# Softmax over two query blocks, head norms over two tiles, and moved steps at the openings of a two-layer decoder trunk

## The chip, the cores and the metric

The kernel runs on one NeuronCore of a Trainium2 chip. The metric is the device time of one launch in microseconds (us). Five engines work beside each other, each in the order of its own queue: TensorE (PE in the profile, with its weight loads as PEld), VectorE (DVE), ScalarE (ACT), GpSimd (POOL) and SyncE (SP), which issues the DMAs. They meet through semaphores.

## The reference

Two layers over 1024 positions and 1024 features, all in float32. Layer 0 mixes with a gated linear recurrence and a matrix memory; layer 1 with sliding-window attention. After each mixer comes a gated feed-forward block with a short convolution, then a gated per-layer embedding. Cut to what the change touches:

```python
def rms_norm(x, g):
    xf = x.astype(jnp.float32)
    y = xf * lax.rsqrt(jnp.mean(xf * xf, axis=-1, keepdims=True) + EPS)
    return (y * g.astype(jnp.float32)).astype(x.dtype)

def banded_sink_attention(q, k, v, sinks):      # q: 16 heads of 64, k and v: 4 heads, blocks of 128 queries
    ...
    logits = jnp.einsum('bnqhgd,bnkhd->bnhgqk', qb, kw) * (dh ** -0.5)
    band = (kj > qi) & (kj <= qi + WINDOW)
    logits = jnp.where(valid[None, :, None, None], logits, -jnp.inf)
    m = jnp.maximum(jnp.max(logits, axis=-1), sink)
    probs = jnp.exp(logits - m[..., None])
    denom = jnp.sum(probs, axis=-1) + jnp.exp(sink - m)
    out = jnp.einsum('bnhgqk,bnkhd->bnhgqd', probs, vw) / denom[..., None]

def reference(...):
    for layer in range(DEPTH):
        h = rms_norm(x, norm_mix[layer])
        mix = rglru_mlstm_mixer(h, ...) if layer % 2 == 0 else swa_sink_mixer(h, positions, ...)
        x = x + mix
        x = x + conv_ffn(rms_norm(x, norm_ffn[layer]), ...)
        gate = jax.nn.sigmoid(rms_norm(x, norm_ple[layer]) @ ple_w_gate[layer])
        x = x + gate * (p[layer] @ ple_w_proj[layer])
```

## The kernel before

Activations lie feature-major: a page is 128 features by 1024 positions, 51 pages are handed out from a free list (`page`, `drop`). Products are made in split precision: every operand is a high part and a low part (`split_cols`: a copy on ACT, a subtraction on DVE or POOL), and a product is three matmuls of 512 columns per 128x128 block of weights. PSUM's eight banks go round in a queue (`bank`, `done`); a bank can be written again when the operation that emptied it is through. The order of the program is the order in which the Python issues it; nothing is rescheduled, and each engine takes its instructions in that order.

**Openings.** `Opening` starts a product group behind an RMS norm while that norm is still being made. `block1`, `norm2` and `block2` prepare the first 512 positions; `run` then issues eight "parts" (12 matmuls each: two pairs of weight tiles, two tiles each, two quarters of the features) and, between them, the second half's statistic `stat(1)` (transposes of the summed squares, a reduce and an inverse square root of about a dozen small DVE operations in `rsqrt`), its `spread(1)` over the partitions, the norms and the blocks 3 and 8. In the kernel before, `stat(1)` stands behind part 2 (counted from 0) and `spread(1)` with all that follows behind part 5, at every opening. After the eight parts come four tiles of two parts each, with the block sums of the fast product scheme (`diff3`, `sum2`, `diffs`) between them, and behind the last of them the blocks 5. The opening is used three times: for layer 0's input projection (with `sums=False`), and for both feed-forward blocks. In the feed-forward block the caller's loop issues the steps of the finished tile after each yield: `s1` (ACT), `s2` (taps on DVE), `s3` (GELU on ACT), `s4` (DVE).

At layer 0, `start` issues the embedding projections and the first half's norm. `first_mid`, called when the blocks 3 and 8 are issued, splits the weights of the eight gate columns (`if_weights`: two casts and two subtractions of 32 columns on DVE) and lets weight making go on. `if_products` follows behind the first finished tile, then `if_cols`, `if_log`, `if_rows`, `if_scan`, `if_rest` and `if_done` at set steps of a slot queue (`later`, `tick`). `constants`, some 30 small DVE operations and three on ACT, stands in slot 4.

**Attention.** The head tiles of `QKV` (128 features: two heads of keys, or one head each of two groups of queries) are made one after another by `qkv_part`, with a `tick` every second of eight steps. Each gets its rotation and its head norm in slots: `rot_a` (evacuation, squares, an exchange of halves by DMA), `rot_s` (transposes and sums of the squares), `rot_b`, `rot_c` (the inverse square root by `rsqrt` for one tile at a time) and, for keys, `rot_k` in slot 6, which waits on PE for the page `rb` that POOL makes in `rot_c`. `attention` is a generator of 32 units (pair of key heads P, half n, block b of 128 queries); `weave` sets one of its steps between the steps of the main products. `scores` of a unit makes the logits of four heads in two banks, folds the window's two halves into 128 columns (`copy_predicated`), takes the maximum, and lets ACT exponentiate head by head with the sum in the same instruction. `normal` (one unit later) adds the sink, takes the reciprocal and multiplies on POOL. `turn` (three units later) transposes on PE and multiplies with two masks on DVE into a page of 1024 columns; `values` (four units later) makes the product with the values.

At the attention's opening two `norm_stat` calls, each with its own chain of small operations, make the row norm `rcol`.

Of the kernel before, what the change touches and what calls it, by code (L numbers as in the profile page):

```python
# [14 lines left out]
ALU = mybir.AluOpType  # L15
# [88 lines left out]
NFIRST, LN, LT, NPOOL, D0, R0, R1 = True, 1, 3, True, 8, 1.0, 1.5  # L104
# [23 lines left out]
class Core:  # L128
# [263 lines left out]
    def rsqrt(self, v, n, name, bufs=2):  # L392

        nc = self.nc
        y = self.small(name + "y", n, bufs=bufs)
        t = self.small(name + "t", n, bufs=bufs)
# [4 lines left out]
        for _ in range(3):  # L401
            nc.vector.tensor_tensor(out=t, in0=y, in1=y, op=ALU.mult)
            nc.vector.scalar_tensor_tensor(out=t, in0=t, scalar=-0.5, in1=v, op0=ALU.mult, op1=ALU.mult)
            nc.vector.scalar_tensor_tensor(out=y, in0=t, scalar=1.5, in1=y, op0=ALU.add, op1=ALU.mult)
        return y
# [25 lines left out]
    def norm_stat(self, h):  # L431
# [10 lines left out]
        return bk, self.rsqrt(v, 4, "n")  # L442

# [242 lines left out]
def layers(ctx: ExitStack, tc: tile.TileContext, a: dict, out: bass.AP, peaks):  # L686
# [157 lines left out]
    def start(op):  # L844
# [21 lines left out]
        for t in pk:  # L866
            c.drop(*t)
        c.ahead = (4, 0)
# [62 lines left out]
    class Opening:  # L931
# [37 lines left out]
        def run(self, p0, p1, extra=None, mid=None, sums=True):  # L969
# [20 lines left out]

            for n, (p, r) in enumerate(tiles):
                p.part(r, 0, 0, True, False)
                if n == 2:
                    self.stat(1)
            for n, (p, r) in enumerate(tiles):
                p.part(r, 0, 1, False, True)
                if n == 1:
                    self.spread(1)
                    self.norm(range(4, 8), 1)
                    self.singles(3, 4, 1)  # L1000
                    c.drop(c.acc, c.sqt)
                    self.norm(range(4), 1)
                    self.singles(8, 0, 1)
                    c.done(self.rows[1])
                    if not sums:
                        c.drop(*self.xs)
                    if mid:
                        mid()
            late = deque([diff3, sum2, diffs] if sums else [])
            for p, r in tiles:  # L1010
# [110 lines left out]
    def if_rest():  # L1121
        ri, rf, rb, rm, rs = (gates[n] for n in ("ri", "rf", "rb", "rm", "rs"))
        gs, bm, ai = rs, ri, rf
        G.tensor_tensor(out=gs[0:4, :], in0=ri[0:4, :], in1=rb[0:4, :], op=ALU.subtract)
        G.tensor_tensor(out=bm[0:4, :], in0=rb[0:4, :], in1=rm[0:4, :], op=ALU.subtract)
# [3 lines left out]
        G.tensor_tensor(out=ai[0:4, :].rearrange("p (b t) -> p b t", t=128),  # L1129
# [305 lines left out]
    def first_mid():  # L1435
        if_weights()
# [397 lines left out]
    def rot_s(key, h):  # L1834

        s = Q["s", key]
        if h == 0:
            Q["v", key] = c.small("qv", 16, bufs=3)
# [3 lines left out]
        V.reduce_sum(out=Q["v", key][:, h * 8:(h + 1) * 8], in_=b.ap.rearrange("p (g d) -> p g d", d=64), axis=AX.X)  # L1842
# [4 lines left out]
    def rot_c(key):  # L1847
# [5 lines left out]
        v3 = v.rearrange("p (b s) -> p b s", s=2)  # L1853
        V.tensor_tensor(out=v3, in0=v3, in1=rcol2.unsqueeze(2).to_broadcast([128, 8, 2]), op=ALU.mult)
        V.tensor_scalar(out=v, in0=v, scalar1=1.0 / 64, scalar2=EPS, op0=ALU.mult, op1=ALU.add)
        y = c.rsqrt(v, 16, "q")
        y3 = y.rearrange("p (b s) -> p b s", s=2)
        r1 = rcol.unsqueeze(2).to_broadcast([128, 8, 2])
# [369 lines left out]
```

## Time and profile before

| | before |
|---|---|
| time, median of three runs | 2450.53 us (2445.98 to 2453.55) |
| the profiled execution's own time | 2450.45 us |
| its span in the trace | 2448.67 us |
| PE busy | 2389.4 us, 98% |
| DVE busy | 1745.3 us, 71% |
| POOL busy | 1336.0 us, 55% |
| ACT busy | 1098.4 us, 45% |
| DMA, mean | 78 GB/s |

Matmuls overlap in the profile: a matmul of 512 columns is shown with about 0.39 us, while the next starts 0.23 us after it. The granted clock (PEclk) is the share of TensorE's full clock in a stretch; it has two levels, 1.2 and 2.4 GHz, so that a stretch with 0.66 holds both.

### The profile page before, as it was taken

Reading aid. Unit: us, or ns where it says so; the run is one execution under the profiler, and the core shown is the slowest. Engines: PE = TensorE matmul, PEld = TensorE weight load, DVE = VectorE, ACT = ScalarE, POOL = GpSimd, SP = SyncE. Lnnn points to the kernel's source line nnn. Section 1 sums busy time; section 2 is a strip of 40 time slices with the busy share of each in tenths; the row PEclk is TensorE's granted clock in tenths of the full one; section 3 lists DMA queues with packets and bytes.
Section 4 is the critical chain, followed back from the end, with each engine's and each line's share of the span. In section 5 each row is a group of like instructions: output and inputs, shape, how many; then the busy total and the mean of one; then the engine's idle time right before and its main releaser. Section 6 shows DMA issues by size and latency. Waiting matters only on the chain. (4 is left out here: it accounts for less than half of the span.)

```text
span 2448.7 us, 29414 instructions
## 1 busy us (share of the span) xinstructions
PE 2389.4 (98%) x10840; PEld 1915.5 (78%) x10840; DVE 1745.3 (71%) x2569; ACT 1098.4 (45%) x1953; POOL 1336.0 (55%) x869
## 2 busy tenths in 40 slices
PE   8899999999999999999999998999999999999999
PEld 6688887877888888888887665687788888888887
DVE  6755555687777666777877888668777777667774
ACT  6474544343434434445452555535344344444441
POOL 0431203237888888888223333332788888888820
PEclk9999999999999999999999999999999999999999
DMA  7121214121111111113233113112111121111323
GB/s 272 36 90 65 78 61 176 57 95 52 52 58 64 53 60 52 52 52 130 95 132 107 31 35 121 65 65 95 52 52 52 54 68 52 61 52 52 120 78 112
DMA packets 57088, 190.18 MB, mean 78 GB/s; under 512 B 6888, under 2 KB 7400, under 8 KB 56944
## 3 DMA queue, kind: packets, MB, share of 16 engines
q1 hardware_dynamic: 56944, 188.31, 22.9%
q8 instruction: 85, 1.39, 0.2%
q14 instruction: 59, 0.48, 0.1%
HBM read 154.69 MB, written 28.34 MB: 75 GB/s over the span
## 5 line engine op out<-in xcount | busy, mean ns | idle before, releaser
L367 POOL TENSOR_TENSOR wp<-wr,wp 128x512 fp32r<-128x512 f32 x462 | 661.8, 1457 | 322.8 <-ACT wp L362 322.8
L502 PE MATMUL pb<-bh,wp 128*128 128x512 f32 x2464 | 614.2, 391 | 10.6 <-ACT u L522 8.6
L502 PEld LDWEIGHTS pb<-bh,wp 128*128 128x128 f32 x2464 | 463.9, 189 | 111.7 <-ACT u L522 9.5
L367 POOL TENSOR_TENSOR wl<-wr,wh 128x1024 fp32r<-128x1024 f32 x78 | 206.3, 2658 | 519.5 <-ACT wh L362 464.2
L616 PE MATMUL pb<-dp,wp 128*128 128x512 f32 x1848 | 457.2, 393 | 3.1 <-DVE dp L603 0.7
L620 DVE TENSOR_TENSOR x<-x,pb 128x512 f32<-128x512 f32 x616 | 398.4, 681 | 46.1 <-PE pb L616 45.9
L616 PEld LDWEIGHTS pb<-dp,wp 128*128 128x128 f32 x1848 | 341.9, 188 | 93.7 <-DVE x L620 13.3
L362 ACT ACTIVATE wp<-wr 128x512 fp32r<-128x512 f32 x462 | 270.9, 622 | 257.9 <-POOL wr L210 192.1
L502 PE MATMUL pb<-bl,wp 128*128 128x512 f32 x1232 | 330.6, 390 | 0.0
L603 DVE TENSOR_TENSOR dp<-fy,dp 128x512 fp32r<-128x512 f32 x154 | 183.2, 1190 | 146.3 <-ACT dp L600 120.7
L502 PEld LDWEIGHTS pb<-bl,wp 128*128 128x128 f32 x1232 | 232.4, 189 | 48.5
L210 POOL TENSOR_TENSOR wr<-wr,wr 128x512 f32<-128x512 f32 x154 | 227.2, 1475 | 8.9 <-DMA wr<-in_down 0.2
L600 ACT ACTIVATE dp<-fy 128x512 fp32r<-128x512 f32 x154 | 96.3, 625 | 266.3 <-DVE fy L593 99.7
L210 POOL TENSOR_TENSOR wr<-wr 128x512 f32<-128x512 f32 x110 | 162.0, 1473 | 47.1 <-DMA wr<-in_up 45.0
L1562 DVE SCALAR_TENSOR_TENSOR fy<-g,params,fy 128x1023 f32<-128x1023 f32 x96 | 156.3, 1628 | 31.9 <-ACT fy L1558 30.2
L383 PE MATMUL pb<-hh,wh 128*128 128x512 f32 x448 | 148.5, 407 | 0.0
L520 DVE TENSOR_TENSOR g<-g,pb 128x512 f32<-128x512 f32 x88 | 58.6, 684 | 125.5 <-PE pb L502 122.2
L549 PE MATMUL pb<-bh,wh 128*128 128x512 f32 x512 | 143.9, 403 | 0.0
L383 PE MATMUL pb<-hl,wh 128*128 128x512 f32 x448 | 142.6, 394 | 0.0
L383 PE MATMUL pb<-hh,wl 128*128 128x512 f32 x448 | 142.2, 393 | 0.0
L549 PE MATMUL pb<-bh,wl 128*128 128x512 f32 x512 | 137.8, 391 | 0.0
L549 PE MATMUL pb<-bl,wh 128*128 128x512 f32 x512 | 137.1, 390 | 0.0
(287 smaller groups left out, 3402.6 us busy)
## 6 DMA issues: line engine op xcount, KB each, us to landing
wr<-in_up SPq DMA_DIRECT2D x96, 512.0 KB, 3.6
wr<-in_down SPq DMA_DIRECT2D x48, 512.0 KB, 3.6
wr<-in_w_in SPq DMA_DIRECT2D x24, 512.0 KB, 5.4
x<-xd SPq DMA_DIRECT2D x24, 512.0 KB, 6.9
ppd<-pp SPq DMA_DIRECT2D x16, 512.0 KB, 3.0
wr<-in_w_out SPq DMA_DIRECT2D x16, 512.0 KB, 5.4
xd<-x SPq DMA_DIRECT2D x32, 256.0 KB, 2.0
wr<-in_gate SPq DMA_DIRECT2D x16, 512.0 KB, 3.8
```

Of the source, the lines that this page charges most:

```text
L210: self.eng(self.w_eng["sum"]).tensor_tensor(out=out, in0=a, in1=b, op=op)
L362: nc.scalar.activation(hi, src, AF.Copy)
L367: self.eng(lo_eng).tensor_tensor(out=lo, in0=src, in1=hi.bitcast(F32), op=ALU.subtract)
L383: self.nc.tensor.matmul(o, lhsT=w, rhs=x[:, c], start=(first and k == 0 and i == 0), stop=(last and k == n - 1 and i == 2))
L502: c.nc.tensor.matmul(bk.ap, lhsT=w[:, o:o + 128], rhs=self.B.t[i][k][q], start=(n == i and k == 0 and j == 0), stop=(k == 3 and j == 2), s ...
L520: c.nc.vector.tensor_tensor(out=out, in0=out, in1=bk.ap, op=ALU.add)
L549: c.nc.tensor.matmul(bk.ap, lhsT=w[n][p], rhs=x[n][q], start=(first and n == 0 and j == 0), stop=(last and n == 3 and j == 2), skip_group_ ...
L600: c.nc.scalar.activation(t[:, lo], src, AF.Copy)
L603: add(out=t[:, hi], in0=src, in1=t[:, lo].bitcast(F32), op=ALU.subtract)
L616: self.c.nc.tensor.matmul(bk.ap, lhsT=p, rhs=q, start=start and j == 0, stop=j == 2, skip_group_check=True)
L620: self.c.nc.vector.tensor_tensor(out=o, in0=o, in1=bk.ap, op=ALU.add)
L1562: V.scalar_tensor_tensor(out=y[:, s:], in0=g[:, :1024 - s], scalar=params[:, o + 2 - s:o + 3 - s], in1=y[:, s:], op0=ALU.mult, op1=ALU.add)
```

## The change

- `Opening.run` has places for the statistic and for what follows it: behind parts 0 and 2 at the feed-forward blocks, behind parts 3 and 5 at layer 0. The blocks 5 are issued ahead of the last yield, so ahead of the caller's steps for the last tile.
- `if_weights` moves from `first_mid` to the end of `start`; `constants` from slot 4 to slot 1; three operations of `if_rest` from POOL to DVE.
- At the attention's opening `norm_whole` makes both halves in one chain and writes `rcol` directly. `rsqrt` can write its last step elsewhere.
- The head norms of two query tiles are made in one chain (`rot_s`, `rot_c`): the even tile leaves its sums, the odd one goes on for both. `rot_k` of the first key tile is in slot 8 instead of 6.
- `scores` of an even block ends with the evacuation; the odd block then does maximum, sinks and exponentials for both. `normal` does nothing for even blocks and both for odd ones (two products on POOL). `turn` multiplies with both masks in one operation of 1024 columns.

```diff
-    def rsqrt(self, v, n, name, bufs=2):
+    def rsqrt(self, v, n, name, bufs=2, out=None, room=None):
...
+            z = y if out is None or i < 2 else out
+            nc.vector.scalar_tensor_tensor(out=z, in0=t, scalar=1.5, in1=y, op0=ALU.add, op1=ALU.mult)
...
+    def norm_whole(self, b, out):
+        nc = self.nc
+        self.sq_finish()
+        v = self.small("qv", 32, bufs=2)[:, :8]
+        for h in range(2):
+            for n in range(4):
+                o = h * 512 + n * 128
+                nc.tensor.transpose(b.b[h].ap[:, n * 128:(n + 1) * 128], self.acc[:, o:o + 128], self.ident)
+            nc.vector.reduce_sum(out=v[:, h * 4:h * 4 + 4], in_=b.b[h].ap.rearrange("p (b f) -> p b f", f=128), axis=AX.X)
+        nc.vector.tensor_scalar(out=v, in0=v, scalar1=1.0 / D, scalar2=EPS, op0=ALU.mult, op1=ALU.add)
+        return self.rsqrt(v, 8, "q", 1, out, 32)
...
         for t in pk:
             c.drop(*t)
+        if_weights()
         c.ahead = (4, 0)
...
-        def run(self, p0, p1, extra=None, mid=None, sums=True):
+        def run(self, p0, p1, extra=None, mid=None, sums=True, at=(0, 2)):
...
+            for n, (p, r, k) in enumerate([(p, r, k) for k in range(2) for p, r in tiles]):
+                p.part(r, 0, k, k == 0, k == 1)
+                if n == at[0]:
+                    self.stat(1)
+                if n == at[1]:
+                    rest()
...
+                if n == 3 and sums:
+                    self.B.drop(8)
+                    self.singles(5, 4, 1)
+                    c.drop(*self.xs[4:])
                 yield p, done
-            if sums:
-                self.B.drop(8)
-                self.singles(5, 4, 1)
-                c.drop(*self.xs[4:])
...
-        G.tensor_tensor(out=gs[0:4, :], in0=ri[0:4, :], in1=rb[0:4, :], op=ALU.subtract)
-        G.tensor_tensor(out=bm[0:4, :], in0=rb[0:4, :], in1=rm[0:4, :], op=ALU.subtract)
+        V.tensor_tensor(out=gs[0:4, :], in0=ri[0:4, :], in1=rb[0:4, :], op=ALU.subtract)
+        V.tensor_tensor(out=bm[0:4, :], in0=rb[0:4, :], in1=rm[0:4, :], op=ALU.subtract)
...
-        G.tensor_tensor(out=ai[0:4, :].rearrange("p (b t) -> p b t", t=128),
+        V.tensor_tensor(out=ai[0:4, :].rearrange("p (b t) -> p b t", t=128),
...
     def first_mid():
-        if_weights()
...
-    later(4, constants)
-    for p, i in op.run(in_pair(pairs0[0], Plain), in_pair(pairs0[1], Plain), gates_start, first_mid, False):
+    later(1, constants)
+    for p, i in op.run(in_pair(pairs0[0], Plain), in_pair(pairs0[1], Plain), gates_start, first_mid, False, (3, 5)):
...
         if key[1] == "q":
             P, _, r = key
-            V.tensor_tensor(out=rq6[:, P, :, r // 2, :, r % 2], in0=y3, in1=r1, op=ALU.mult)
+            if r % 2 == 0:
+                Q["vv", P] = v
+                return
+            n = 2
...
+        y = c.rsqrt(v, 16 * n, "q", 1, None, 32)
...
-                later(6, lambda: rot_k(key))
+                later(6 if key[0] else 8, lambda: rot_k(key))
...
-    st = [c.norm_stat(h) for h in range(2)]
+    b = c.wide()
+    c.norm_whole(b, rcol)
+    c.done(b)
...
+            st[u] = cb, st["cb"]
+            if b % 2 == 0:
+                return
+            cv = st["cb"].rearrange("p (b h k) -> p b h k", b=2, h=4)
...
+            V.reduce_max(out=m3, in_=cv, axis=AX.X)
+            V.scalar_tensor_tensor(out=m3, in0=m3, scalar=-1.0, in1=rr, op0=ALU.mult, op1=ALU.mult)
+            V.tensor_tensor(out=m4, in0=m4, in1=nk, op=ALU.min)
+            V.tensor_tensor(out=e4, in0=sk, in1=m4, op=ALU.add)
+            for z in range(2):
+                for h in range(4):
+                    A.activation(cv[:, z, h, :], cv[:, z, h, :], AF.Exp, bias=m3[:, z, h:h + 1], scale=rr[:, z, h:h + 1],
+                                 accum_out=sm[:, 4 * z + h:4 * z + h + 1])
...
         def normal(u):
+            if u[2] % 2 == 0:
+                return
+            cv, sm, es = st.pop("s")
             V.tensor_tensor(out=sm, in0=sm, in1=es, op=ALU.add)
             V.reciprocal(out=sm, in_=sm)
-            (G if NPOOL else V).tensor_tensor(out=cv, in0=cv, in1=sm.unsqueeze(2).to_broadcast([128, 4, 128]), op=ALU.mult)
+            for z in range(2):
+                G.tensor_tensor(out=cv[:, z], in0=cv[:, z], in1=sm[:, 4 * z:4 * z + 4].unsqueeze(2).to_broadcast([128, 4, 128]),
+                                op=ALU.mult)
...
             if b:
-                V.tensor_tensor(out=pt[:, 512:1024].rearrange("p (h q) -> p h q", h=4), in0=p3,
-                                in1=cs["prevT"].unsqueeze(1).to_broadcast([128, 4, 128]), op=ALU.mult)
+                V.tensor_tensor(out=pt.rearrange("p (z h q) -> p z h q", z=2, h=4), in0=p3.unsqueeze(1).to_broadcast([128, 2, 4, 128]),
+                                in1=masks.rearrange("p (z q) -> p z q", z=2).unsqueeze(2).to_broadcast([128, 2, 4, 128]),
+                                op=ALU.mult)
```

## Rows read from the trace of the kernel before

**Rows 1.** The page: span, and busy us (share of the span) xinstructions of the engines.
```profile
span 2448.7 us, 29414 instructions
PE 2389.4 (98%) x10840; PEld 1915.5 (78%) x10840; DVE 1745.3 (71%) x2569; ACT 1098.4 (45%) x1953; POOL 1336.0 (55%) x869
```

**Rows 2.** PE's waits, who ended them: us in total, times, longest us.
```profile
PE pb L502 <- ACT u L522: 8.6, 2, 4.3
PE pb L2004 <- DVE pt L2012: 6.5, 3, 2.6
...
PE pb L1064 <- DVE wif L367: 5.3, 2, 3.9
PE pb L1873 <- POOL rb L1865: 4.9, 1, 4.9
PE pb L438 <- DVE acc L422: 3.1, 2, 1.6
PE pb L2028 <- DVE pt L2009: 2.4, 1, 2.4
PE pb L1104 <- DVE tab L1095: 1.9, 1, 1.9
...
PE pb L1140 <- POOL rs L1124: 1.3, 1, 1.3
```

**Rows 3.** Stretches: length, busy us (xinstructions) by engine, granted clock, DMA share, GB/s.
```profile
63.00:71.50 8.50, 3.65 (x10) 0.92 (x8) 8.43 (x4) 3.45 (x5) 8.50 (x4) 0.80 0.00 0
110.00:116.00 6.00, 4.68 (x26) 3.93 (x26) 5.96 (x5) 0.00 (x0) 5.84 (x3) 0.72 0.01 3
512.00:522.00 10.00, 5.69 (x16) 4.16 (x15) 6.92 (x8) 5.17 (x9) 3.33 (x2) 0.66 0.80 292
900.00:950.00 50.00, 49.88 (x219) 40.54 (x218) 34.97 (x46) 21.42 (x36) 41.94 (x30) 1.00 0.16 53
1316.00:1328.00 12.00, 7.05 (x27) 6.01 (x27) 11.14 (x29) 0.00 (x0) 6.52 (x3) 0.72 0.23 87
1340.00:1525.00 185.00, 170.72 (x910) 116.30 (x910) 151.12 (x374) 95.92 (x321) 61.25 (x40) 0.97 0.21 63
1679.00:1689.50 10.50, 6.20 (x17) 4.58 (x17) 7.31 (x9) 5.17 (x9) 3.33 (x2) 0.67 0.76 287
```

**Rows 4.** Timeline, first feed-forward opening: start, us, engine, line, op, out<-in, idle before.
```profile
465.06 0.69 DVE L422 TENSOR_TENSOR acc<-acc,sq 128x512 f32<-128x512 f32 x1 [0.16 <-ACT sq L420]
465.09 1.07 PE L549 MATMUL pb<-bh,wh 128*128 128x512 f32 x4
...
479.80 2.72 DVE L948 SCALAR_TENSOR_TENSOR x<-x,params,pb 128x512 f32<-128x512 f32 x4 [5.54 <-PE pb L448]
...
510.40 2.61 DVE L1562 SCALAR_TENSOR_TENSOR fy<-g,params,fy 128x1023 f32<-128x1023 f32 x2
...
513.10 1.06 ACT L1567 ACTIVATE fy<-fy 128x1024 f32<-128x1024 f32 x1 [4.22 <-DVE fy L1562]
...
516.14 0.57 ACT L522 ACTIVATE u<-pb 128x512 f32<-128x512 f32 x1
```

**Rows 5.** Timeline, first opening: the gate weights' split, and POOL beside it.
```profile
61.96 9.89 POOL L367 TENSOR_TENSOR wl<-wr,wh 128x1024 fp32r<-128x1024 f32 x4 [29.00 <-ACT wh L362]
62.59 2.37 DVE L366 CAST wif<-tab 128x32 fp32r<-128x32 f32 x1
```

**Rows 6.** Timeline of POOL at the attention's opening.
```profile
1319.46 1.87 POOL L1865 TENSOR_SCALAR rb<-qy 128x1024 f32<-128x1024 f32 x1 [10.99 <-DVE qy L1863]
```

**Rows 7.** DVE by lines, 1340 to 1560 us: xcount | busy us, mean ns | idle before.
```profile
L1982 DVE TENSOR_REDUCE mx<-cb 128x4 f32<-128x512 f32 x30 | 20.6, 686 | 1.0
...
L1986 DVE TENSOR_TENSOR es<-params,mx 128x4 f32<-128x4 f32 x30 | 15.6, 520 | 1.0
...
L402 DVE TENSOR_TENSOR qt<-qy 128x16 f32<-128x16 f32 x21 | 3.7, 175 | 0.7
```

**Rows 8.** ACT by lines, 1340 to 1560 us.
```profile
L1988 ACT ACTIVATE cb<-cb,mx,tab 128x128 f32<-128x128 f32 x120 | 57.9, 483 | 91.3 <-DVE mx L1985 91.3
```

More of the change, by code (lines that the diff above doesn't have):

```diff
@@ L390, in wk @@
                 for k in range(n)]
-    def rsqrt(self, v, n, name, bufs=2):
+    def rsqrt(self, v, n, name, bufs=2, out=None, room=None):
         nc = self.nc
-        y = self.small(name + "y", n, bufs=bufs)
-        t = self.small(name + "t", n, bufs=bufs)
+        y = self.small(name + "y", room or n, bufs=bufs)[:, :n]
+        t = self.small(name + "t", room or n, bufs=bufs)[:, :n]
         nc.vector.tensor_scalar(out=t.bitcast(I32), in0=v.bitcast(I32), scalar1=1, scalar2=None,
@@ L400, in rsqrt @@
                                 op0=ALU.mult, op1=ALU.add)
-        for _ in range(3):
+        for i in range(3):
             nc.vector.tensor_tensor(out=t, in0=y, in1=y, op=ALU.mult)
             nc.vector.scalar_tensor_tensor(out=t, in0=t, scalar=-0.5, in1=v, op0=ALU.mult, op1=ALU.mult)
-            nc.vector.scalar_tensor_tensor(out=y, in0=t, scalar=1.5, in1=y, op0=ALU.add, op1=ALU.mult)
-        return y
+            z = y if out is None or i < 2 else out
+            nc.vector.scalar_tensor_tensor(out=z, in0=t, scalar=1.5, in1=y, op0=ALU.add, op1=ALU.mult)
+        return z
     def sq_begin(self, eng="dve"):
@@ L989, in diffs, with rest @@
                 self.singles(4, 4, 0)
-            for n, (p, r) in enumerate(tiles):
[L992 to L1010, printed above, removed]
+            def rest():
+                self.spread(1)
+                self.norm(range(4, 8), 1)
+                self.singles(3, 4, 1)
+                c.drop(c.acc, c.sqt)
+                self.norm(range(4), 1)
+                self.singles(8, 0, 1)
+                c.done(self.rows[1])
+                if not sums:
+                    c.drop(*self.xs)
+                if mid:
+                    mid()
+            for n, (p, r, k) in enumerate([(p, r, k) for k in range(2) for p, r in tiles]):
[4 more added lines that the diff above has]
+                    rest()
+            late = deque([diff3, sum2, diffs] if sums else [])
+            for n, (p, r) in enumerate(tiles):
                 p.part(r, 1, 1, True, False)
@@ L1836, in rot_s @@
         s = Q["s", key]
+        second = key[1] == "q" and key[2] % 2
         if h == 0:
-            Q["v", key] = c.small("qv", 16, bufs=3)
+            Q["v", key] = (Q.pop(("vv", key[0])) if second else c.small("qv", 32, bufs=2))
+        v = Q["v", key][:, 16 * second:16 * second + 16]
         b = c.bank()
@@ L1982, in scores @@
-            V.reduce_max(out=mx, in_=cv, axis=AX.X)
-            V.scalar_tensor_tensor(out=mx, in0=mx, scalar=-1.0, in1=rr, op0=ALU.mult, op1=ALU.mult)
-            m3, e3 = (t.rearrange("p (s r) -> p s r", s=2) for t in (mx, es))
-            V.tensor_tensor(out=m3, in0=m3, in1=nk, op=ALU.min)
-            V.tensor_tensor(out=e3, in0=sk, in1=m3, op=ALU.add)
-            for h in range(4):
-                A.activation(cv[:, h, :], cv[:, h, :], AF.Exp, bias=mx[:, h:h + 1], scale=rr[:, h:h + 1],
-                             accum_out=sm[:, h:h + 1])
+            sk, nk = (t[:, o + 8 * P:o + 8 * P + 8].rearrange("p (s n r) -> p s n r", s=2, n=2)[:, :, n, :].unsqueeze(1)
+                      .to_broadcast([128, 2, 2, 2]) for t, o in ((params, o), (negs, 0)))
@@ L1999, in turn @@
         def turn(u):
             b = u[2]
-            cb, page = st[u][0], st[u][4]
+            cb, page = st[u]
             bk = c.bank()
@@ L2044, in attention @@
         for i in range(n + LT + 2):
-            if NFIRST and 0 <= i - LN < n:
+            if 0 <= i - LN < n:
                 normal(un[i - LN])
@@ L2049, in attention @@
                 yield
-            if not NFIRST and 0 <= i - LN < n:
-                normal(un[i - LN])
             if 0 <= i - LT < n:
```

42 lines of the change are left out of this document (22 added, 20 removed).

## The prediction

> **What bounds the kernel now.** First the page: TensorE (PE) is busy 2389.4 of 2448.7 us, and no other engine is above 71% [rows 1]. So the change can take nothing from the matmul work. It can only remove time in which PE stands (2448.7 - 2389.4 = 59 us) or in which it runs slowly. Then the waits of PE, to see who ends the 59 us: eight rows name 38 us of it, nearly all small waits for VectorE (DVE), ScalarE (ACT) or GpSimd (POOL) at the openings and in the attention [rows 2]. Then the stretches around those waits: the granted clock is 1.00 in undisturbed work and 0.66 to 0.97 where PE has just stood [rows 3], a mix of the two levels (1.2 and 2.4 GHz). A removed wait therefore pays twice, if the clock then stays up. An undisturbed matmul costs 49.88/219 = 0.228 us [rows 3]; a "part" of an opening is 12 matmuls, 2.74 us. Last the timeline of three places. The profiled execution took 2450.45 us (span 2448.67), the median of three is 2450.53, so the sum is made against 2450.45.
>
> **First opening.** (1) The weight split of the gate products moves from behind the norms to the end of start(). Now four DVE operations of 32 columns take 2.37 us each, in step with four POOL operations of 9.89/4 = 2.47 us that begin just before [rows 5]; DVE is held while POOL works on SBUF. POOL had been idle 29 us before them [rows 5], so at the new place the four cost about the 0.175 us of a small DVE operation [rows 7], under 1 us in all, ahead of a statistic that waits for nothing of theirs but the queue. Gone: 5.3 us of waits [rows 2] and the slow clock: 10 matmuls took 3.65 us instead of 2.28, 1.4 us [rows 3]. (2) The second statistic one part later: one of the two L438 waits, 1.5 us [rows 2]; the other is in the first statistic and stays. The row statistic then has two parts (5.5 us) until its rows are spread, and needs about 13 small DVE operations of 0.2 us plus one reduce of 0.686 [rows 7], 3.3 us: covered. (3) constants() three steps earlier takes some 30 small operations from in front of the gates' logarithm: 1.9 us (L1104) [rows 2]. Its new neighbours are the POOL operations at 61.96, so it may itself be held up to their end; PE needs the result over 10 us later. (4) Three 4x1024 operations go from POOL to DVE: 1.3 us (L1140) [rows 2], and the clock of 110 to 116 us, at most 6 x (1 - 0.72) = 1.7, taken as 1.5 [rows 3]. They queue ahead of the convolution taps, which POOL holds up today; I set the two against each other. Sum 5.3 + 1.4 + 1.5 + 1.9 + 1.3 + 1.5 = 12.9 us, bounds 8 and 13.1.
>
> **The two feed-forward openings.** PE stands twice 4.3 us for ACT's copy of u (L522) [rows 2], and 16 and 17 matmuls then take 5.69 and 6.20 us instead of 3.65 and 3.88: 2.0 + 2.3 us of clock [rows 3]. The row of the copy shows why: it starts at 516.14, behind four block copies, behind a GELU at 513.10 that waits for DVE's taps (510.40 + 2.61) [rows 4], the end of a DVE queue that has run almost without a break since the first norm at 479.80. The change spreads the statistic after part 2 instead of part 5, so that queue starts 3 x 2.74 = 8.2 us earlier, and it puts the last four block copies ahead of the GELU. The copy of u must end by about 512.4 (4.3 before 516.7), so the GELU must start by 510.8, 2.3 us earlier. Some of the 8.2 is lost where DVE then waits for PE's own parts, but 2.3 should survive; what is late next is those four copies, which need the last part and end about when the GELU should start, so I leave 0.5 us a time. The added cost is plain: the statistic now comes after part 0, which ends at 465.09, while the last sum of squares lands at 465.06 + 0.69 = 465.75 [rows 4]: PE waits 0.7 us, twice. Sum 8.6 + 4.3 - 1.4 - 1.0 = 10.5 us; bounds 0 (the wait re-forms) and 11.5.
>
> **The attention's opening.** norm_whole does both halves in one chain and drops 14 small operations; the key's page of scales (L1865, 1319.46 [rows 6]) comes earlier, and its transposes are asked for two steps later (5.5 us). PE's 4.9 us for it [rows 2] go by either alone. The first scores come a whole tile later and are the cover. Clock of 1316 to 1328: at most 12 x 0.28 = 3.4, at least 7.05 - 27 x 0.228 = 0.9 [rows 3]; most of the 27 are short transposes, so nearer the first: 2.4. Sum 7.3 us, bounds 5.8 and 8.3.
>
> **The attention.** From 1340 to 1525 PE stands 185 - 170.72 = 14.3 us, and 3% of the clock is 5.5 us [rows 3]: 19.8 to win. The waits are for PSUM banks that DVE frees late (L2012, L2009 [rows 2]); DVE is busy 151.12 of 185 [rows 3] and serves everything in order. The change removes per pair of query blocks five small operations, joins two reduces and twice two mask products; per two query tiles 13 small ones of the head norms. A small one costs 0.175 + 0.03 = 0.2 us [rows 7]: 16 x 5 x 0.2 + 3 x 13 x 0.2 = 24 us. The joined ones save a start each, of which no row has the price alone; at least 0, at most 0.2 each for 16 + 28 of them, 9 us; I take 4. And L1986 shows a mean of 0.520 for four columns against 0.175 for sixteen [rows 7], so it is held by POOL as in rows 5; half as many are exposed. DVE so falls from 82% to about 66% busy.
> What the change adds is a longer chain: an odd block's scores must pass two evacuations, one reduce of at most 2 x 0.686, three small ones, eight exponentials of 0.483 [rows 7, 8] = 3.9 us, two small ones: some 7 us, before the next even block's evacuation, which is queued behind the sum on DVE. Thirty units lie in 220 us [rows 7], 7.3 us each, so that evacuation is about on time, but the pair's first block, which has three units between scores and transpose, now has two after its pair is complete: 14.6 us against 7 plus two normalisations on POOL. A burst of head-norm work or a held DVE still fits, not both. I therefore count 9 of 19.8 us; bounds 0 and 19.8.
> A rule that speaks against it: the Trainium skill (Perfetto Trace Analysis, Optimizing Scalar/DVE Operations) says that where Vector is not saturated but causes bubbles on other engines, breaking instructions up may let work finish sooner; this change groups them. No row decides it; it is the first rival. The same section gives about 60 ns overhead for a DVE operation on SBUF; by that, as an estimate, the 119 small ones would be worth 7 us of DVE instead of 24, and the attention some 3 us instead of 9, 2417 in all; the 0.2 us of the rows is what I use.
>
> **Sum.** 12.9 + 10.5 + 7.3 + 9 = 39.7 us; 2450.45 - 39.7 = 2411 us.
>
> **The rivals.** (A) The pair's chain eats what DVE gains: waits move from L2012 to the transposes waiting for POOL's normalisation, attention 0: 2420. For: the room shrinks from three units to two. Against: DVE's load falls by some 28 us. (B) The feed-forward wait re-forms, behind the four block copies or the weights: 2411 + 10.5 = 2421.5; with A 2430. (C) All waits named go and the clock stays up: 12.9 + 11.5 + 8.3 + 19.8 = 52.5, 2398. (D) Waits go but PE stays idle often enough that the clock falls as before: the clock terms (1.4 + 1.5 + 4.3 + 2.4 + half of 5.5) come back, 12.4: 2423. (E) The later stages give it back: in the feed-forward blocks POOL is busy 41.94 of 50 us [rows 3]; if weights are made by POOL's own pace, not as pages come free, PE only waits there: 2446 to 2451. Against: at 99.8% busy PE there sets the pace [rows 3]. (F) Slower: the pair's chain becomes the pace. It takes 7 us plus POOL of the 14.6 that the transposes allow; if DVE's other work and POOL's holds add more than about 8 us in every pair, PE waits over (39.7 - 9 + 7.4)/16 = 2.4 us a pair more than now, and the time passes 2458. Such a sum is seen today only behind head-norm bursts, in a few places.
>
> **How the numbers follow.** About 0.3% (7.4 us) is what a measurement can tell from no change. Forecast 0.48, A 0.18, B 0.12 (with A 0.02 more), C 0.10, D 0.03: all faster, 0.93. E 0.04: same. F 0.03: slower. The range of 8 in 10 runs from C's 2399 to 2428, past A, B and D, and leaves out A with B, E and F.
>
> **What would show it.** Right: no L1064, L1873, L1104 or L1140 among PE's waits; clock 1.00 around 65, 112 and 1320 us; two new L438 waits of 0.7 us; the L522 waits under 1 us; DVE busy near 120 in the attention's 185 us. Wrong: L2004 waiting for POOL cb L1997 many times over (A, F); an L502 wait of 3 us or more at an opening (B); new waits for POOL's weights between 550 and 1150 us (E).

## The result, and the profile after

The changed kernel took 2409.47 us (median of five runs, 2408.38 to 2410.60) against 2447.55 us for the kernel before on the same chip (2445.98 to 2453.55): a ratio of 0.9839, with a 95% interval of 0.9825 to 0.9854. The forecast was 2411 us. The profiled execution took 2410.05 us with a span of 2408.3.

The page of the changed kernel, span and engines, against [rows 1]:

```profile
span 2408.3 us, 29214 instructions
PE 2376.0 (99%) x10840; PEld 1907.8 (79%) x10840; DVE 1689.8 (70%) x2382; ACT 1094.7 (45%) x1937; POOL 1329.1 (55%) x866
```

PE has the same 10,840 matmuls. Its busy time fell by 13.4 us, its standing time from 59 to 32 us, together 40.4 us of the two spans. The first is the clock: the same matmuls at the higher level more of the time. So about a third of the gain was clock, and two thirds waits that are gone.

PE's waits in the changed kernel, against [rows 2] (us in total, times, longest us):

```profile
PE pb L383 <- ACT ph L362: 7.1, 2, 6.2
PE pb L1984 <- DVE cb L1998: 2.3, 2, 1.7
PE pb L2066 <- DVE pt L2046: 2.1, 1, 2.1
PE pb L2040 <- DVE pt L2046: 1.5, 1, 1.5
PE pb L2040 <- POOL cb L2032: 1.3, 1, 1.3
PE pb L439 <- DVE acc L423: 1.2, 2, 0.6
```

Lines have moved: L438 is now L439, L502 is L516, L522 is L536, L1873 is L1899, L2004 is L2040, L2028 is L2066, and the mask product L2009 and L2012 is L2046. None of the waits that the prediction named at the openings is left. The attention's waits for masks are not gone but smaller: 1.5 us (L2040) for 6.5, and 2.1 us (L2066) for 2.4. The largest row is the start of the program, which the change does not touch. The two L439 waits of 0.6 us are the ones that the prediction expected to be new.

Stretches of the changed kernel at the places of [rows 3] (length, busy us (x) of PE, PEld, DVE, ACT, POOL, granted clock, DMA share, GB/s):

```profile
62.00:70.50 8.50, 8.50 (x38) 3.64 (x36) 8.43 (x10) 5.30 (x10) 8.50 (x4) 1.00 0.00 0
99.00:105.00 6.00, 6.00 (x39) 4.86 (x38) 5.89 (x10) 2.27 (x3) 0.00 (x0) 1.00 0.36 109
496.00:506.00 10.00, 10.00 (x45) 8.27 (x45) 7.87 (x11) 7.30 (x13) 3.94 (x3) 1.00 0.69 257
900.00:950.00 50.00, 49.89 (x219) 40.61 (x218) 38.63 (x47) 21.74 (x36) 39.52 (x28) 1.00 0.17 53
1298.00:1310.00 12.00, 12.00 (x63) 10.08 (x62) 9.09 (x12) 2.04 (x3) 9.91 (x4) 1.00 0.25 86
1308.00:1493.00 185.00, 178.44 (x979) 123.78 (x977) 127.91 (x268) 95.39 (x312) 67.40 (x42) 0.99 0.21 63
1642.00:1652.00 10.00, 10.00 (x46) 8.29 (x45) 7.90 (x13) 6.00 (x11) 5.15 (x4) 1.00 0.90 340
```

In every opening PE is busy for the whole stretch at clock 1.00, where before it stood for a fifth to over a half of it and the clock was 0.66 to 0.80. In the attention's 185 us it is busy 178.44 us instead of 170.72.

Where the time went, by stage. Every kernel here issues the same 10,840 matmuls, so the start of the matmul with the same number can be compared. The borders are matmuls 150, 1000, 2738, 5900, 7304 and 7771 (us; gains are taken before rounding):

| stage (matmuls) | before | after | gain | forecast |
|---|---|---|---|---|
| layer-0 opening (150 to 1000) | 187.3 | 175.4 | 11.9 | 12.9 |
| first feed-forward opening (1000 to 2738) | 385.6 | 379.4 | 6.3 | 10.5 for both |
| attention's opening (2738 to 5900) | 725.3 | 717.2 | 8.1 | 7.3 |
| attention (5900 to 7304) | 282.0 | 272.8 | 9.1 | 9 |
| second feed-forward opening (7304 to 7771) | 115.2 | 110.1 | 5.1 | (above) |
| rest (7771 to the last) | 702.1 | 702.0 | 0.1 | 0 |

The attention's stage in the two kernels, from matmul 5900 to matmul 7304:

```profile
1343.30:1625.20 281.90, 267.62 (x1405) 187.30 (x1404) 220.33 (x514) 143.08 (x450) 103.73 (x67) 0.98 0.20 66
1317.20:1590.00 272.80, 263.29 (x1405) 185.97 (x1404) 181.23 (x351) 140.41 (x434) 106.27 (x67) 0.99 0.21 68
```

For the same matmuls PE stands 9.5 us instead of 14.3 and is busy 4.3 us less, so half of the 9.1 us gained here is clock. DVE is busy 39 us less.

### The profile page after: what moved, and what is told of

It reads as the page before. It is cut to its first block, busy times and chain, and to the rows that moved or that the text cites. A ratio compares the mean times of both kernels' runs of the same rounds, so it can differ in the third digit from the quotient of the medians.

```text
span 2408.3 us, 29214 instructions
## 1 busy us (share of the span) xinstructions
PE 2376.0 (99%) x10840; PEld 1907.8 (79%) x10840; DVE 1689.8 (70%) x2382; ACT 1094.7 (45%) x1937; POOL 1329.1 (55%) x866
## 5 line engine op out<-in xcount | busy, mean ns | idle before, releaser
L367 POOL TENSOR_TENSOR wp<-wr,wp 128x512 fp32r<-128x512 f32 x462 | 662.2, 1458 | 303.7 <-ACT wp L362 303.7
L516 PE MATMUL pb<-bh,wp 128*128 128x512 f32 x2464 | 610.6, 390 | 2.3 <-POOL wp L367 1.1
L516 PEld LDWEIGHTS pb<-bh,wp 128*128 128x128 f32 x2464 | 461.8, 188 | 102.0 <-ACT wp L362 2.9
L367 POOL TENSOR_TENSOR wl<-wr,wh 128x1024 fp32r<-128x1024 f32 x78 | 205.7, 2650 | 491.8 <-ACT wh L362 436.6
L516 PE MATMUL pb<-bl,wp 128*128 128x512 f32 x1232 | 329.3, 389 | 0.0
L516 PEld LDWEIGHTS pb<-bl,wp 128*128 128x128 f32 x1232 | 231.2, 188 | 48.1
```

What stands on the lines that cost most here:

```text
L367: self.eng(lo_eng).tensor_tensor(out=lo, in0=src, in1=hi.bitcast(F32), op=ALU.subtract)
L516: c.nc.tensor.matmul(bk.ap, lhsT=w[:, o:o + 128], rhs=self.B.t[i][k][q], start=(n == i and k == 0 and j == 0), stop=(k == 3 and j == 2), s ...
```

## The experiments

Each kernel is the changed kernel with one part undone or altered. A difference from the changed kernel is (its ratio - 0.9839) x 2447.6 us, so that chips cancel; an interval of a ratio is about ±0.0015, 3.6 us, so that a difference of two is known to about 5 us. Beside it stands the difference by stage in the profiled execution, from the numbered matmuls as above. Kernels that leave the attention alone still differ there by -0.1 to +2.0 us, so less than 2 us is not read into that stage, and in the second feed-forward opening by 0 to -1.0 us. In the other stages of the table such kernels agree within 0.3 us.

| kernel | us | ratio (95%) | against after, us | stage of the trace, us |
|---|---|---|---|---|
| u_open | 2423.67 | 0.9899 (0.9884 to 0.9913) | +14.7 | opening +12.6, attention +1.8 |
| u_ffn | 2421.35 | 0.9888 (0.9874 to 0.9903) | +12.0 | first +6.2, second +4.5, attention +2.0 |
| u_stat | 2417.30 | 0.9867 (0.9850 to 0.9883) | +6.9 | first +3.4, second +2.6, attention +1.5 |
| u_qkv | 2415.73 | 0.9867 (0.9851 to 0.9884) | +6.9 | attention's opening +6.8 |
| u_slot | 2412.95 | 0.9850 (0.9834 to 0.9864) | +2.7 | attention's opening +4.6 |
| u_whole | 2410.02 | 0.9836 (0.9821 to 0.9851) | -0.7 | attention's opening +0.2 |
| u_soft | 2419.66 | 0.9883 (0.9869 to 0.9898) | +10.8 | attention +10.6 |
| u_heads | 2419.54 | 0.9879 (0.9864 to 0.9894) | +9.8 | its opening +1.6, attention +9.8 |
| u_soft_heads | 2417.97 | 0.9869 (0.9852 to 0.9885) | +7.3 | its opening +1.7, attention +6.7 |
| u_masks | 2410.36 | 0.9840 (0.9826 to 0.9855) | +0.2 | attention +0.7 |
| v_at13 | 2408.96 | 0.9832 (0.9817 to 0.9847) | -1.7 | first -0.6, second -1.0, attention +2.0 |
| v_both | 2410.26 | 0.9840 (0.9825 to 0.9855) | +0.2 | first -0.7, second -1.1, attention +4.9, rest +1.4 |

### The layer-0 opening undone: u_open

```diff
-        if_weights()
         c.ahead = (4, 0)
...
     def first_mid():
+        if_weights()
...
-    later(1, constants)
-    for p, i in op.run(in_pair(pairs0[0], Plain), in_pair(pairs0[1], Plain), gates_start, first_mid, False, (3, 5)):
+    later(4, constants)
+    for p, i in op.run(in_pair(pairs0[0], Plain), in_pair(pairs0[1], Plain), gates_start, first_mid, False, (2, 5)):
...
-        V.tensor_tensor(out=gs[0:4, :], in0=ri[0:4, :], in1=rb[0:4, :], op=ALU.subtract)
-        V.tensor_tensor(out=bm[0:4, :], in0=rb[0:4, :], in1=rm[0:4, :], op=ALU.subtract)
+        G.tensor_tensor(out=gs[0:4, :], in0=ri[0:4, :], in1=rb[0:4, :], op=ALU.subtract)
+        G.tensor_tensor(out=bm[0:4, :], in0=rb[0:4, :], in1=rm[0:4, :], op=ALU.subtract)
...
-        V.tensor_tensor(out=ai[0:4, :].rearrange("p (b t) -> p b t", t=128),
+        G.tensor_tensor(out=ai[0:4, :].rearrange("p (b t) -> p b t", t=128),
```

> The changed kernel with layer 0's opening as before (gate weights split in first_mid, constants in slot 4, the three operations of if_rest on POOL, the second statistic behind part 2). Theory (each removed wait pays with its slow clock): 2409.5 + 12 = 2421 to 2422 us, the waits L1064, L1104 and L1140 and one of 1.5 us for the statistic are back, and the granted clock falls again near 65 and 112 us; nothing changes after that. Rival (most of this came from the statistic alone, or the later stages give it back): 2411 to 2415.

PE's waits of this kernel, from 40 to 120 us:

```profile
PE pb L1080 <- DVE wif L367: 6.1, 2, 3.9
PE pb L1120 <- DVE tab L1111: 1.9, 1, 1.9
PE pb L439 <- DVE acc L423: 1.4, 1, 1.4
PE pb L1156 <- POOL rs L1140: 1.3, 1, 1.3
```

All four named waits come back, 10.7 us where the prediction counted 10.0, and the opening is 12.6 us longer. The mechanism of the weight split holds too: at its new place its two casts take 0.175 and 0.176 us and its two subtractions 0.191 and 0.195, where the kernel before shows 2.37 us for the first of them [rows 5] and 2.27 to 2.39 for the others.

### The feed-forward openings: u_ffn and u_stat

u_ffn undoes both edits, u_stat only the first, the place of the statistic; the second puts block 5's copies ahead of the GELU:

```diff
-        def run(self, p0, p1, extra=None, mid=None, sums=True, at=(0, 2)):
+        def run(self, p0, p1, extra=None, mid=None, sums=True, at=(2, 5)):
...
-                if n == 3 and sums:
-                    self.B.drop(8)
-                    self.singles(5, 4, 1)
-                    c.drop(*self.xs[4:])
                 yield p, done
+            if sums:
+                self.B.drop(8)
+                self.singles(5, 4, 1)
+                c.drop(*self.xs[4:])
```

> The changed kernel with both feed-forward openings as before (statistic behind part 2, the rest behind part 5, blocks 5 behind the last yield). Theory (PE waits for ACT's copy of u at the end of DVE's queue): two waits of 4.3 us with a slow clock are back, the two waits of 0.6 us for the statistic are gone: 2409.5 + 11.5 = 2421. Rival (the wait is set by the weights, not by DVE's queue): under 4 us more, 2410 to 2413.

> The changed kernel with the feed-forward openings' statistic behind part 2 and its rest behind part 5 again, but the blocks 5 still ahead of the last yield. Theory (DVE's queue starts too late, the statistic is what matters): 8 to 12 us more, 2417 to 2421, the waits for ACT's copy of u still near 4 us. Rival (the four block copies ahead of that copy are what matters): 2409 to 2412.

u_ffn has the old wait for u again, twice 4.3 us, with the clock low behind the first (0.66 from 501 to 511 us). In u_stat, where neither the theory nor the rival came true, half of it is left:

```profile
PE pb L516 <- ACT u L536: 8.6, 2, 4.3
```
```profile
PE pb L516 <- ACT u L536: 4.5, 2, 2.2
```

ACT's timeline at the first opening, u_stat:

```profile
496.16 2.18 ACT L485 ACTIVATE bh<-x 128x512 fp32r<-128x512 f32 x4
500.47 1.06 ACT L1583 ACTIVATE fy<-fy 128x1024 f32<-128x1024 f32 x1 [2.13 <-DVE fy L1578]
```

and of the changed kernel:

```profile
496.52 2.18 ACT L485 ACTIVATE bh<-x 128x512 fp32r<-128x512 f32 x4
498.60 1.05 ACT L1583 ACTIVATE fy<-fy 128x1024 f32<-128x1024 f32 x1
```

With block 5's copies early but the statistic late, ACT stands 2.13 us after the copies until DVE's taps are done, and the copy of u behind it is 2.2 us late for PE, twice. With both edits the GELU follows the copies at once and the copy of u is in time. So the order on ACT takes one half of the old 4.3 us and the earlier DVE queue the other; by subtraction the block copies are worth some 5 us and the statistic some 6 to 7. The copies were not put back alone.

### The attention's opening: u_qkv, u_slot and u_whole

u_qkv undoes both hunks, u_slot the first, u_whole the second:

```diff
-                later(6 if key[0] else 8, lambda: rot_k(key))
+                later(6, lambda: rot_k(key))
```
```diff
-    b = c.wide()
-    c.norm_whole(b, rcol)
-    c.done(b)
+    st = [c.norm_stat(h) for h in range(2)]
     c.drop(c.acc, c.sqt)
+    for h in range(2):
+        V.tensor_copy(rcol[:, 4 * h:4 * h + 4], st[h][1])
+        c.done(st[h][0])
```

> The changed kernel with the attention's opening as before (two norm_stat chains, the first key tile's rot_k in slot 6). Theory (PE waits for POOL's page rb, 4.9 us and a slow clock): 2409.5 + 8 = 2417 to 2418. Rival (the head norms made for two tiles already free DVE enough that rb comes in time): 2410 to 2412.

> The changed kernel with rot_k of the first key tile in slot 6 again, norm_whole kept. The prediction said that either of the two alone takes the wait for rb away: then 2409 to 2411 and no L1899 wait for POOL rb. Rival (the one chain brings rb forward by less than the 4.9 us): a wait of 1 to 4 us with a slow clock, 2411 to 2415.

> The changed kernel with the two separate row statistics ahead of the attention again, but the key's transposes still asked for two steps later (8). With both undone the wait was 5.0 us and the time 6.3 us longer; with the slot alone undone it was 2.7 us and the time 2 to 3 us longer. Theory: two steps are 5.5 us of TensorE's work, so the slot alone covers the whole wait: no wait at the scales' transposes, 0 to 1 us. Rival: each half covers only about half, and a wait of 2.3 us stays, with 1.7 us of clock: 2 to 4 us.

The wait of u_qkv, then that of u_slot; u_whole has none at these transposes:

```profile
PE pb L1899 <- POOL rb L1891: 5.0, 1, 5.0
```
```profile
PE pb L1899 <- POOL rb L1891: 2.7, 1, 2.7
```

POOL's page of scales in u_slot, in u_whole and in the changed kernel:

```profile
1297.56 1.88 POOL L1891 TENSOR_SCALAR rb<-qy 128x1024 f32<-128x1024 f32 x1 [8.85 <-DVE qy L1889]
```
```profile
1301.45 1.87 POOL L1891 TENSOR_SCALAR rb<-qy 128x1024 f32<-128x1024 f32 x1 [11.19 <-DVE qy L1889]
```
```profile
1299.20 1.87 POOL L1891 TENSOR_SCALAR rb<-qy 128x1024 f32<-128x1024 f32 x1 [8.95 <-PE pb L1859]
```

The page starts 2.25 us later in u_whole than in the changed kernel, as the two separate statistics cost, and still ends at 1303.32, a microsecond before the transposes that read it at 1304.3. So asking two steps later covers all of the wait. The joined statistic alone takes off 2.3 of 5.0 us (u_slot: the wait of 2.7 and some 2 us of clock make the 4.6 of its trace), and beside the later slot it brings nothing: u_whole is as fast as the changed kernel. So that either alone would do, as the theory had it for u_slot, is refuted. These two edits make 6.8 of the 8.1 us gained in this stage; the head norms of two tiles bring the rest, since with them undone it is 1.6 us (u_heads) and 1.7 us (u_soft_heads) longer.

### The attention, softmax and head norms: u_soft, u_heads, u_soft_heads, u_masks

u_soft takes one query block at a time again, u_heads one tile of head norms, u_soft_heads both (with its small tiles of 16 columns), u_masks makes the two mask products one by one.

```diff
...
-            if b % 2 == 0:
-                return
-            cv = st["cb"].rearrange("p (b h k) -> p b h k", b=2, h=4)
...
-            mx, es, sm = c.small("mx", 8, bufs=3), c.small("es", 8, bufs=3), c.small("dn", 8, bufs=2)
+            mx, es, sm = c.small("mx", 4, bufs=5), c.small("es", 4, bufs=5), c.small("dn", 4, bufs=5)
...
-            V.reduce_max(out=m3, in_=cv, axis=AX.X)
+            V.reduce_max(out=mx, in_=cv, axis=AX.X)
...
```

That is u_soft's core; u_heads:

```diff
-        second = key[1] == "q" and key[2] % 2
+        second = 0
...
-            if r % 2 == 0:
-                Q["vv", P] = v
-                return
-            n = 2
...
```

and u_masks:

```diff
...
-                V.tensor_tensor(out=pt.rearrange("p (z h q) -> p z h q", z=2, h=4), in0=p3.unsqueeze(1).to_broadcast([128, 2, 4, 128]),
...
+                V.tensor_tensor(out=pt[:, 512:1024].rearrange("p (h q) -> p h q", h=4), in0=p3,
+                                in1=cs["prevT"].unsqueeze(1).to_broadcast([128, 4, 128]), op=ALU.mult)
```

> The changed kernel with the softmax of one query block at a time, head norms and masks as changed. Theory (DVE's queue is relieved of about 16 us): 4 to 6 us slower, 2414 to 2416, DVE busy in the attention about 15 us more, PE's waits for banks (turn's masks) longer. Rival (the longer chain of a pair costs what it saves, so breaking it up again is no loss): 2405 to 2411.

> The changed kernel with the head norms of one tile at a time again (39 small DVE operations more in the attention, 8 us of DVE). Theory (every microsecond of DVE's queue counts alike): a third to a half of what the softmax cost when it was undone, 2412 to 2415. Rival (only what POOL holds up, and what stands in the softmax's own chain, counts): 2408 to 2411.

> The changed kernel with two mask products of 512 columns each again. From the traces: one of 1024 columns takes 1.217 us, two of 512 take 0.68 + 0.60 us; so 28 x 0.07 = 2 us of DVE. Theory: 2409 to 2411, no more than can be measured. Rival (the page of probabilities is complete later, PE's value products wait): 2412 to 2415.

> The changed kernel with both the softmax one query block at a time and the head norms one tile at a time (joined masks and all the openings as changed). Alone, the first cost 10 us and the second 8 to 10. Theory: the two relieve the same queue on VectorE and only both together take the attention's waits away, so without both the attention is as in the kernel before: 8 to 12 us above the changed kernel, ratio 0.988 to 0.990. Rival: the two are separate gains that add, 18 to 20 us above the changed kernel, ratio 0.992 (about 2429 on the first chip).

The masks do nothing, as expected. The other two each cost about twice what was expected, yet both together cost no more than either: 6.7 us in the attention, against 10.6 and 9.8, where the sum would be 20.4. They do not add. That both together cost less than one alone is not shown, since the intervals of the times overlap. To see why, first DVE by lines in the changed kernel, 1312 to 1532 us, against [rows 7]:

```profile
L2014 DVE TENSOR_REDUCE mx<-cb 128x8 f32<-128x1024 f32 x16 | 19.5, 1220 | 0.5
...
L2016 DVE TENSOR_TENSOR mx<-mx,tab 128x8 f32<-128x8 f32 x16 | 6.9, 430 | 0.5
...
L2015 DVE SCALAR_TENSOR_TENSOR mx<-mx,tab 128x8 f32<-128x8 f32 x16 | 5.2, 325 | 0.5
...
L2017 DVE TENSOR_TENSOR es<-params,mx 128x8 f32<-128x8 f32 x16 | 2.7, 167 | 0.5
```

and in u_soft, 1314 to 1538 us:

```profile
L2009 DVE TENSOR_REDUCE mx<-cb 128x4 f32<-128x512 f32 x31 | 21.3, 686 | 1.1
...
L2010 DVE SCALAR_TENSOR_TENSOR mx<-mx,tab 128x4 f32<-128x4 f32 x31 | 14.0, 450 | 1.1
L2013 DVE TENSOR_TENSOR es<-params,mx 128x4 f32<-128x4 f32 x31 | 13.6, 438 | 1.1
L2012 DVE TENSOR_TENSOR mx<-mx,tab 128x4 f32<-128x4 f32 x31 | 10.6, 341 | 1.1
```

The three small operations of the softmax take 6.9 + 5.2 + 2.7 = 14.8 us joined and 14.0 + 13.6 + 10.6 = 38.2 us apart. Undisturbed they would take 16 x 3 x 0.167 = 8.0 and 31 x 3 x 0.167 = 15.5. The rest, 6.8 and 22.7 us, is time in which POOL holds them: of DVE's operations of at most 64 columns between matmuls 5900 and 7304, 5 in the changed kernel and 24 in u_soft last over 0.3 us, and every one of them runs beside a POOL operation and ends within 0.06 us of it. A single case in the changed kernel, from its timeline:

```profile
1464.98 2.37 POOL L1846 TENSOR_TENSOR qe<-qe,cos 128x1024 f32<-128x1024 f32 x1
1465.15 2.23 DVE L2016 TENSOR_TENSOR mx<-mx,tab 128x8 f32<-128x8 f32 x1
...
1469.82 1.22 DVE L2046 TENSOR_TENSOR pt<-pb,tab 128x1024 f32<-128x1024 f32 x1
...
1471.09 1.26 PE L2066 MATMUL pb<-pt,v 128*64 128x256 f32 x8 [2.11 <-DVE pt L2046]
```

Eight columns take 2.23 us and end with POOL's rotation at 1467.35. DVE's queue is then 2 us late, the mask at 1469.82 stands in it without a break and is late with it, and PE stands 2.11 us: the largest wait that the attention still has. The Trainium skill (SBUF — State Buffer, Who interferes with whom) states the rule: a VectorE operation with two SBUF inputs, or in a two-port mode, and a GpSimd operation that reads SBUF exclude each other, and whichever is issued second blocks until the first ends. The trace agrees: the operation above is held, and the reduce L2014, which the Trainium skill's page excepts, never is. Its 16 instances take 1.220 to 1.222 us, though nine of them start while POOL works.

Now u_heads. Its softmax is joined, but its head norms come twice as often. Its timeline at the first wait of 2 us:

```profile
1345.18 2.38 POOL L367 TENSOR_TENSOR wl<-wr,wh 128x1024 fp32r<-128x1024 f32 x1 [1.09 <-ACT wh L362]
1345.29 2.29 DVE L1877 TENSOR_SCALAR qv<-qv 128x16 f32<-128x16 f32 x1
1347.51 2.39 POOL L1846 TENSOR_TENSOR qe<-qe,cos 128x1024 f32<-128x1024 f32 x1
1347.62 2.31 DVE L397 TENSOR_SCALAR qt<-qv 128x16 int32<-128x16 int32 x1
...
1349.97 0.17 DVE L399 TENSOR_SCALAR qy<-qt 128x16 int32<-128x16 int32 x1
...
1352.15 0.76 DVE L1993 COPY_PREDICATED cb<-tab,pb 128x256 f32<-128x256 int32 x2
1352.64 1.42 PE L1979 MATMUL pb<-qe,qe 64*128 64x256 f32 x6 [2.07 <-DVE cb L1993]
```

One burst of head norms, two of its operations held, occupies DVE from 1345.29 to 1352.2, and the evacuation of the scores stands behind it. The waits by line in this stage, u_soft, u_heads, and u_soft_heads:

```profile
PE pb L2031 <- DVE pt L2037: 7.7, 3, 2.8
```
```profile
PE pb L1979 <- DVE cb L1993: 6.5, 4, 2.1
```
```profile
PE pb L2026 <- DVE pt L2032: 4.3, 3, 2.2
PE pb L2052 <- DVE pt L2032: 2.4, 2, 2.1
```

With the softmax apart, PE waits for masks. With the softmax joined and the norms apart, it waits four times for the evacuation of scores. Two of these waits (0.7 and 1.6 us) are those of the changed kernel; the two of 2.1 us are new, and in front of each stands a norm burst with two of its operations held (L1877 and L397 above, L403 and L405 from 1470.34 to 1474.99). Waits are not the whole cost: between matmuls 5900 and 7304 PE stands 9.5 us in the changed kernel, 17.5 in u_soft, 13.8 in u_heads and 13.1 in u_soft_heads. The rest of the differences, some 2.6, 5.5 and 3.2 us, is clock: in u_heads it is down at four places of this stage (0.83 from 1350 to 1360 us; 0.76 over 7 us from 1474, 1488 and 1522 on), in the changed kernel at one (0.76 from 1469 to 1476).

DVE's load does not order these kernels. In their 224 us it is busy 160.25 us in u_heads, 172.87 in u_soft and 185.86 in u_soft_heads, and the least loaded of the three is no faster than the most loaded. What does order them is in part where a hold falls. In u_soft the last operation of a joined norm burst (L1885) meets POOL's L367, and a mask stands behind it:

```profile
1433.49 2.45 DVE L1885 TENSOR_TENSOR tab<-qy,rcol 128x16 f32<-128x16 f32 x2
...
1437.22 0.63 PE L2031 MATMUL pb<-cst,cb 128*128 128x128 f32 x4 [2.51 <-DVE dn L2022]
```

In u_soft_heads the shorter burst is over at this place and the mask has started (1433.20) when the same POOL operation begins (1433.35), and PE does not stand. In u_heads it is the head norms that POOL catches; the three small operations of the softmax take 8.4 us there, hardly more than undisturbed. That both have to be joined because only then a burst is rare enough for the pair's longer chain is a reading of these timelines. The cost of each combination is measured; its cause is inferred, and no run moves the holds alone.

### Two attempts at a faster version: v_at13 and v_both

v_at13 has the first of these edits, v_both both:

```diff
-        def run(self, p0, p1, extra=None, mid=None, sums=True, at=(0, 2)):
+        def run(self, p0, p1, extra=None, mid=None, sums=True, at=(1, 3)):
...
-LN, LT, D0, R0, R1 = 1, 3, 8, 1.0, 1.5
+LN, LT, D0, R0, R1 = 1, 3, 8, 1.0, 1.2
```

> The changed kernel with the feed-forward openings' row statistic one part later: behind parts 1 and 3 instead of 0 and 2. Theory: the two waits of 0.6 us for the last sum of squares go, and the copy of u still comes in time, because three parts of delay (8.2 us) gave waits of 2.2 us, so one part (2.7 us) gives none: 1.1 us less, 2407 to 2409 on the first chip. Rival: the copy of u is on time by less than one part, and its wait returns with 0.5 to 2 us each and the clock: 1 to 5 us more.

> As the kernel with the statistic one part later, and in the output projection that is woven with the second half of the attention 1.2 attention steps for each projection step instead of 1.5. Theory: the waits for VectorE that are left there (2.1, 1.5 and 0.8 us near 1470 to 1487 us, and 1.7 us of clock) get more matmul work between them and go: 4 to 5 us less, about 2404 on the first chip. Rival: the attention steps that are left over run bare at the end of the projection, and TensorE waits there for VectorE by 5 us or more: 2412 or more.

In v_at13 the two 0.6 us waits go and the copy of u is still in time, as its theory said. The openings are 0.6 and 1.0 us shorter, but in the second, kernels that leave it alone differ by as much. The attention gave 2.0 us back in the profiled execution, and the time (ratio 0.9832, 0.9817 to 0.9847) can't be told from that of the changed kernel. In v_both theory and rival both missed: the waits between 1468 and 1487 us shrink, but new ones appear (the longest 2.3 us, L439 behind DVE's sum of squares at the next opening), the trace is 4.9 us longer in the attention, and the time is the same within its interval. Spreading the attention wider seems to have pushed DVE's work towards the next opening; only the place of the new waits says so.

## Why the prediction was right, step by step

- **Layer-0 opening, 12.9 us.** Right: 11.9 by stage (12.6 by undoing it), all four waits and the clock. The constants at their new place are in part held, as the prediction allowed: four of their small operations take 2.0 to 2.4 us each beside POOL's work from 61.7 to 71.8 us. Neither they nor the three operations moved to DVE make a new wait of PE.
- **Feed-forward openings, 10.5 us.** Slightly low: 6.3 + 5.1 = 11.4, its upper bound of 11.5. The statistic's new waits were 0.6 us each, for 0.7. The 0.5 us a time kept back for the last four copies were not needed. The 2.3 us that the prediction asked of the earlier queue, with the copies out of the way, are what u_stat then showed (2.2 us left). What was generous is the lead: the taps end at 498.02 us in the changed kernel and at 500.38 in u_stat, 3.2 us earlier when counted from the same matmul (2040), so most of the 8.2 us is lost on the way. The expectation of u_stat, waits near 4 us, left out what the copies alone bring.
- **Attention's opening, 7.3 us.** The size is right (8.1), one sentence is wrong: "PE's 4.9 us for it go by either alone". The later slot does it alone, the joined statistic does not (2.7 us left in u_slot). The step that failed is the lead that the page of scales gains: 14 small operations at 0.2 us are 2.8 us, and 2.25 was measured, less than the 4.9 to be covered.
- **Attention, 9 of 19.8 us.** Measured 9.1, but that is luck: the 9 was a pick between the bounds 0 and 19.8 and not worked out from DVE's load. What the step missed is that PE's gain is not proportional to that load: the pieces do not add, and each alone is worth nothing (u_heads and u_soft are no faster than u_soft_heads).
- **DVE's load in the attention, 28 us.** It fell by more than forecast: over the same matmuls by 39 us (220.33 to 181.23) for a forecast of 24 for 119 small operations and 4 for the joined ones. There are indeed 119 operations of at most 64 columns fewer (151 for 270), and they take 34.3 us instead of 71.4. Of these 37 us, 18 are held time: what lies above 0.175 us in the operations that last over 0.3 us falls from 25.7 to 7.4 us. The prediction named the holds, took them to halve and gave them no number; this is the term that was left at nothing. The joined reduce and masks were worth the small end of their bounds: 21.3 - 19.5 = 1.8 us of DVE for the reduce, nothing measurable for the masks. In the 185 us DVE is busy 127.91, where near 120 was named: the 28, counted for all 16 pairs, was taken off a stretch that holds only a part of them.
- **Rivals.** B did not come: no wait for u. D did not: the clock stayed at 1.00 in the openings. E did not: 49.89 of 50 us busy in the feed-forward stretch, as before, and the rest of the kernel moved by 0.1 us. C, all of 52.5 us, was missed mainly in the attention, 9.1 of 19.8 us. A holds for the joined softmax without the joined norms: with the head norms left as they were (u_heads against u_soft_heads) it brings nothing, and the waits move. They moved to the scores' evacuation, not to POOL's normalisation as A had it; that wait (L2040 for L2032) is there once, 1.3 us. The rule of the Trainium skill behind A (Perfetto Trace Analysis, Optimizing Scalar/DVE Operations: break instructions up where Vector is unsaturated but causes bubbles) would let the ungrouped softmax do better. u_soft, with all else as in the changed kernel, is 10.6 us worse in this stage. The 60 ns overhead of the same section of the Trainium skill gave the prediction's estimate of 7 us of DVE. It lost 39, because a small operation takes 0.17 us even undisturbed, and because 5 are held instead of 24.
- **A reading that is wrong.** The eight rows of [rows 2] add up to 34.0 us, not 38. No term of the sum uses it.

## What to carry to other kernels

Read a removed wait together with the clock behind it: about a third of the 40 us was matmuls that ran at the higher level again. Where a queue has slack on average and still makes waits, do not price its edits by its load: find the bursts and the operations that another engine holds, and expect two edits on the same queue to be worth nothing alone and something together, so test them apart and together. Tiny VectorE operations beside GpSimd work on SBUF cost up to a whole GpSimd operation each (2.2 to 2.4 us here), so that joining them paid 37 us of VectorE's time, almost twice their undisturbed duration.

## What the runs showed of the hardware

A small DVE operation held by POOL ends with POOL's operation even if it has 16 columns and one input: L1877 and L397 in u_heads took 2.29 and 2.31 us, where the next of their kind took 0.17.

The clock's fall is not a function of the wait in front of it alone. PE waits 1.67 us for the evacuation L1998, until 1512.93, in the changed kernel, and 1.63 us for the same one, until 1513.05, in v_at13, and the granted clock of the 7 us around it is, first in the changed kernel, then in v_at13:

```profile
1511.00:1518.00 7.00, 5.33 (x31) 3.58 (x30) 6.83 (x16) 2.05 (x6) 4.38 (x3) 1.00 0.01 2
```
```profile
1511.00:1518.00 7.00, 5.37 (x20) 3.58 (x18) 6.84 (x14) 2.18 (x5) 4.38 (x3) 0.76 0.01 2
```

31 matmuls lie in the one stretch and 20 in the other: 7 x (1 - 0.76) = 1.7 us lost. That is most of the 2 us by which the attention differs between kernels that are the same there. Near 1475 us it is the other way round: behind the same wait of 2.1 us (L2066 for L2046) the clock from 1469 to 1476 us is 0.76 in the changed kernel and 1.00 in v_at13. That difference evens out, because v_at13 then waits 3.0 us for the next mask and the changed kernel 1.5. What decides whether the clock falls, the runs do not show.
